# Selecting the top keys of the indexer: two of its passes over a tile moved to ScalarE, and two VectorE passes merged into one

## The chip, the cores and the metric

The kernel runs on one core of one Trainium2 chip. The metric is the device time of one execution in microseconds (us). A core has five engines that work side by side, each through its own queue in order: TensorE (PE in the rows, its weight loads PEld), VectorE (DVE), ScalarE (ACT), GpSimd (POOL) and SyncE (SP), which issues the transfers between HBM and the on-chip memory. An instruction that waits for another engine holds up everything behind it on its own queue.

## The reference

One decoder block over 1024 positions of width 1024. What matters here is the sparse branch. An indexer scores every key for every query, each query keeps its 256 best admissible keys, and attention runs over those alone:

```python
iscore = jnp.where(causal[None], iscore, -jnp.inf)
_, sel = lax.top_k(iscore, topk)          # topk = 256, ties: the lower index first
...
logits = jnp.where(valid[:, None], logits, -jnp.inf)
p = jax.nn.softmax(logits, axis=-1)
```

Beside it stand the forgetting attention ("fox", eight heads), the projections of x, two gates of 1024 columns each, an MLP of width 4096 and norms.

## The kernel before

The program is written as a list of stages, and a scheduler orders each engine's instructions by its own simulated times. What is written in one place of the program may so run among the work of another, and a change of a few instructions can reorder all that comes after it.

After the norm and the indexer's scores come 16 heads, first the eight fox heads (`n` = 0 to 7) and then the eight sparse ones. Each turn of the loop over heads holds `attention` of head n, the projection `proj_qk` (and `proj_v`) of the next head, and one or two `gate_tile` calls (table `GC`), which are pure matrix work that nothing needs soon. All matrix work goes through line L75 (`mm`); its results in the PSUM tile `g` are projections, those in `S` are attention scores, those in `pv` are probabilities times values. Transposes of probabilities go to `ptr` (L583).

The selection finds, for each query, the 256th largest score by bisection. The score is cut into a high and a low half of 16 bits each. During heads 0 to 7 `bisect_step` counts how many keys lie above a threshold, 4 bits per head; the three widest of the six key tiles are counted on ScalarE (`AF.Sign` with an accumulator, L495), the others on VectorE (L498). Query tiles 2 to 7 take part, and tile i has W = 128 (i + 1) columns, so W is 384, 512, 640, 768, 896 or 1024.

When the last bit is known, at the end of turn n = 7, `select_tile` (L521 to L535) turns each tile into a mask that holds 0 for a chosen key and 1e30 for any other. `sel[i]` holds the low halves (`L`), `isc[i]` the high ones (`hi`), `Thi`, `Tlo` the threshold, `need` the number of ties to take. `bjunk` (called `gt`) and `eqt` (`eq`) are scratch tiles of which there is one each, so the six tiles follow one another. Its passes over a tile, all on VectorE, are: L527 counts low halves above the threshold, L529 and L531 mark ties, L530 marks what is above, L532 numbers the ties in order (a running sum), L533 keeps the first `need` of them, L534 adds both marks, L535 makes the mask. L528 works on one column. The masks are first read by the sparse heads.

The scheduler interleaves these with what the fox heads want of VectorE: L563 reads attention scores out of `S` (out to `sp`, `mn`), L592 adds up a head's result from `pv` (`yt`), L585 makes the low part of transposed probabilities (`pl`), L318 and L325 read out projections (`QB`, `KA`). GpSimd meanwhile splits weights into a high and a low part (L120, L123).

Of the kernel before, what the change touches and what calls it, by code (L numbers as in the profile page):

```python
# [16 lines left out]
AF = mybir.ActivationFunctionType  # L17
ALU = mybir.AluOpType
# [14 lines left out]
BIG = 1.0e30  # L33
# [24 lines left out]
def block_kernel(ctx: ExitStack, tc: tile.TileContext, x, c, w_ada, b_ada, g_norm1, w_in, b_forget,  # L58
                 rel_bias, w_bf, w_bd, w_out, g_norm2, w_mlp1, w_mlp2, g_final, onehot, out):
    nc = tc.nc  # L60
# [49 lines left out]
    def split_w(pieces, lo_eng=None, kt=KT, dst=None):  # L110
        st = stg.tile([P, 1024], F32, name="st", tag="st")
        view = st.rearrange("p (k c) -> p k c", k=kt)
        for d0, d1, src in pieces:
            nc.sync.dma_start(view[:, :, d0:d1], src)
        return split_st(st, lo_eng, dst)
# [50 lines left out]
    isc, sel = [None, None], [None, None]  # L166
# [299 lines left out]
    cnt = pA.tile([P, NQ], F32, name="cnt")  # L466
    goal = pA.tile([P, NQ], F32, name="goal")
    nct = pA.tile([P, NQ], F32, name="nct")
# [52 lines left out]
    def select_tile(i):  # L521
        q, W = i - 2, (i + 1) * P
        hi = isc[i].bitcast(I16)[:, 1::2]
        L = sel[i].bitcast(U16)
        th, tl, nd = Thi[:, q:q + 1], Tlo[:, q:q + 1], need[:, q:q + 1]
        gt, eq = bjunk[:, :W], eqt[:, :W]
        nc.vector.tensor_scalar(gt, L, tl, None, op0=ALU.is_gt, op1=ALU.add, accum_out=cnt[:, q:q + 1])  # L527
        nc.vector.tensor_tensor(nd, nd, cnt[:, q:q + 1], op=ALU.subtract)  # L528
        nc.vector.tensor_scalar(eq, L, tl, None, op0=ALU.is_equal)  # L529
        nc.vector.scalar_tensor_tensor(gt, hi, th, gt, op0=ALU.is_gt, op1=ALU.add)  # L530
        nc.vector.scalar_tensor_tensor(eq, hi, th, eq, op0=ALU.is_equal, op1=ALU.mult)  # L531
        nc.vector.tensor_tensor_scan(out=L, data0=eq, data1=eq, initial=0.0, op0=ALU.add, op1=ALU.max)  # L532
        nc.vector.scalar_tensor_tensor(eq, L, nd, eq, op0=ALU.is_le, op1=ALU.mult)  # L533
        nc.vector.tensor_tensor(gt, gt, eq, op=ALU.add)  # L534
        nc.vector.tensor_scalar(sel[i], gt, -BIG, BIG, op0=ALU.mult, op1=ALU.add)  # L535


    def attention(kind, h, qk, V, Yd=None):
# [190 lines left out]
    for n, (kind, h) in enumerate(heads):  # L729
# [19 lines left out]
        if n == NH - 1:  # L749
            for i in range(2, NTT):  # L750
                select_tile(i)
# [23 lines left out]
    for half in range(2):  # L775
        sl = slice(half * 512, half * 512 + 512)
        for cp in range(4):
            hi, lo = split_w([(0, 256, wbv[1][:, :, cp * 256:cp * 256 + 256])], nc.gpsimd, 4)
            hv, lv = hi.rearrange("p (k c) -> p k c", k=4), lo.rearrange("p (k c) -> p k c", k=4)
            for c2 in range(2):  # L780
                ct, cs = 2 * cp + c2, slice(c2 * P, c2 * P + P)
                gt = pY.tile([P, 512], F32, name="gt2", tag="gt2", bufs=3)
# [22 lines left out]
    with ExitStack() as st4:  # L805
# [6 lines left out]
        for ch in range(2):  # L812
# [3 lines left out]
            for t in range(NTT):  # L816
                hf, tl = t // 4, slice((t % 4) * P, (t % 4) * P + P)
# [398 lines left out]
```

## Time and profile before

| | |
|---|---|
| median of 3 runs | 1632.06 us (1631.8 to 1632.16) |
| profiled execution, its own time | 1634.09 us |
| its span, first to last instruction | 1632.2 us |
| TensorE busy | 1565.2 us, 96% of the span |
| VectorE busy | 1150.7 us, 71% |
| ScalarE busy | 947.4 us, 58% |
| GpSimd busy | 747.9 us, 46% |
| mean granted clock of TensorE | 0.984 of full speed |

The profiled execution is one run more, and it is about 2 us longer than the median of the others. "Busy" of TensorE counts a matmul until its modelled end, and matmuls overlap, so it says when the engine has nothing to do and not how well it works. The selection lies at 430 to 500 us of the span.

### The profile page before, as it was taken

Reading aid. Unit: us, or ns where it says so; the run is one execution under the profiler, and the core shown is the slowest. Engines: PE = TensorE matmul, PEld = TensorE weight load, DVE = VectorE, ACT = ScalarE, POOL = GpSimd, SP = SyncE. Lnnn points to the kernel's source line nnn. Section 1 sums busy time; section 2 is a strip of 40 time slices with the busy share of each in tenths; the row PEclk is TensorE's granted clock in tenths of the full one; section 3 lists DMA queues with packets and bytes.
Section 4 is the critical chain, followed back from the end, with each engine's and each line's share of the span. In section 5 each row is a group of like instructions: output and inputs, shape, how many; then the busy total and the mean of one; then the engine's idle time right before and its main releaser. Section 6 shows DMA issues by size and latency. Waiting matters only on the chain.

```text
span 1632.2 us, 22837 instructions
## 1 busy us (share of the span) xinstructions
PE 1565.2 (96%) x7585; PEld 1300.7 (80%) x7585; DVE 1150.7 (71%) x2230; ACT 947.4 (58%) x1689; POOL 747.9 (46%) x628
## 2 busy tenths in 40 slices
PE   4989999999989999999999998999999989999998
PEld 3777788887878888888888887888888868888887
DVE  6787777878897665567767547765555475758988
ACT  4454899898747777677663136554544343533433
POOL 3432222333335565656545301886666564343730
PEclk8999999999999999999999999999999989999999
DMA  9321222132124443544878456454444579655862
GB/s 301 81 47 51 61 79 57 44 80 49 53 63 147 116 138 100 155 139 142 304 242 292 126 187 215 141 167 152 151 142 143 181 287 344 231 207 193 268 222 103
DMA packets 223870, 253.01 MB, mean 155 GB/s; under 512 B 49137, under 2 KB 136257, under 8 KB 223753
## 3 DMA queue, kind: packets, MB, share of 16 engines
q1 hardware_dynamic: 215112, 233.73, 45.5%
q10 hardware_dynamic: 8640, 17.83, 2.9%
q8 instruction: 60, 0.98, 0.3%
q14 instruction: 58, 0.47, 0.1%
HBM read 186.48 MB, written 65.03 MB: 154 GB/s over the span
## 4 chain that ended last, share of the span: by engine, by line
PE 73%; DVE 10%; ACT 9%; DMA 4%; issue 2%; SPq 1%; POOL 1%; ACTq 0%; DVEq 0%; POOLq 0%
PE g L75 31%; PE S L75 24%; PE tr L75 8%; PE pv L75 7%; ACT eqt L495 4%; PE ptr L583 2%; ACT sp L567 1%; DVE acc L252 1%; DMA wap<-in_w_ada_dram 1%; ACT sp L570 1%; ACT ph L584 1%; DVE sp L563 1%; DVE pl L585 1%; DVE isc L434 1%; DMA gt<-G_d 1%
## 5 line engine op out<-in xcount | busy, mean ns | idle before, releaser
L75 PE MATMUL g<-h_hi,whi 128*128 128x512 f32 x656 | 264.5, 403 | 8.4 <-DVE KA L325 5.4
L75 PE MATMUL g<-h_hi,wlo 128*128 128x512 f32 x656 | 262.7, 400 | 0.0
L75 PE MATMUL g<-h_lo,whi 128*128 128x512 f32 x656 | 262.5, 400 | 0.0
L1039 DVE TENSOR_TENSOR ut<-rw,ut 128x1024 fp32r<-128x1024 f32 x112 | 182.0, 1670 | 66.3 <-ACT ut L1038 66.2
L123 POOL TENSOR_TENSOR wlo<-st,whi 128x1024 fp32r<-128x1024 f32 x60 | 148.6, 2477 | 110.7 <-ACT whi L122 103.0
L1038 ACT ACTIVATE ut<-rw 128x1024 fp32r<-128x1024 f32 x112 | 112.0, 1052 | 144.7 <-PE pv L75 66.6
L1053 POOL TENSOR_TENSOR rw<-rw 128x1024 f32<-128x1024 f32 x40 | 117.6, 2943 | 125.5 <-DMA rw<-in_w_mlp_dram 114.2
L75 PEld LDWEIGHTS g<-h_hi,whi 128*128 128x128 f32 x656 | 125.2, 191 | 34.1 <-issue 5.5
L75 PEld LDWEIGHTS g<-h_hi,wlo 128*128 128x128 f32 x656 | 124.7, 190 | 24.3
L75 PEld LDWEIGHTS g<-h_lo,whi 128*128 128x128 f32 x656 | 124.9, 190 | 22.5
L75 PE MATMUL S<-ut 128*128 128x512 f32 (+1 forms) x576 | 138.4, 385 | 0.0
L75 PEld LDWEIGHTS S<-ut 128*128 128x128 f32 x576 | 106.9, 191 | 21.2 <-DVE ut L1039 0.2
L585 DVE TENSOR_TENSOR pl<-ptr,ph 128x512 fp32r<-128x512 f32 (+1 forms) x160 | 99.8, 631 | 23.6 <-ACT ph L584 21.7
L567 ACT ACTIVATE sp<-sp,mn 128x128 f32<-128x128 f32 (+7 forms) x128 | 98.5, 771 | 25.5 <-DVE mn L563 25.2
L584 ACT ACTIVATE ph<-ptr 128x512 fp32r<-128x512 f32 (+1 forms) x160 | 86.4, 550 | 42.5 <-PE ptr L583 40.5
L495 ACT ACTIVATE eqt<-sel_all,nct 128x768 bf16<-128x768 int16 (+5 forms) x99 | 102.5, 1035 | 9.9 <-DVE nct L491 8.5
L570 ACT ACTIVATE sp<-sp,mn 128x128 f32<-128x128 f32 (+7 forms) x128 | 96.9, 770 | 18.6 <-DVE mn L569 18.1
L75 PE MATMUL g<-ut 128*128 128x512 f32 (+1 forms) x384 | 94.6, 381 | 6.0 <-ACT ut L1038 4.6
L583 PE MATMUL ptr<-ident,sp 128*128 128x128 f32 x576 | 89.8, 272 | 1.6 <-DVE nct L491 1.2
L122 ACT ACTIVATE whi<-st 128x1024 fp32r<-128x1024 f32 x51 | 53.8, 1055 | 62.3 <-DMA st<-in_w_mlp_dram 18.5
L75 PE MATMUL pv<-ph,V 128*128 128x256 f32 x320 | 85.2, 285 | 3.1 <-DVE yt L592 3.1
L75 PEld LDWEIGHTS g<-ut 128*128 128x128 f32 x384 | 70.0, 191 | 20.5 <-ACT ut L1038 5.0
(436 smaller groups left out, 3922.5 us busy)
## 6 DMA issues: line engine op xcount, KB each, us to landing
rw<-in_w_mlp_dram SPq DMA_DIRECT2D x72, 512.0 KB
rw<-U_d SPq DMA_DIRECT2D x56, 512.0 KB
wap<-in_w_ada_dram SPq DMA_DIRECT2D x64, 256.0 KB
st<-in_w_mlp_dram SPq DMA_DIRECT2D x32, 512.0 KB
st<-in_w_in_dram SPq DMA_DIRECT2D x26, 512.0 KB
U_d<-cc SPq DMA_DIRECT2D x48, 256.0 KB
st<-in_w_in_dram SPq DMA_DIRECT2D x33, 256.0 KB
G_d<-t SPq DMA_DIRECT2D x32, 256.0 KB
```

Of the source, the lines that this page charges most:

```text
L75: nc.tensor.matmul(o, l, r, start=start, stop=stop)
L122: nc.scalar.activation(hi, st, AF.Copy)
L123: (lo_eng or nc.vector).tensor_tensor(lo, st, hi.bitcast(F32), op=ALU.subtract)
L495: nc.scalar.activation(eqt[:, :(i + 1) * P], sel[i].bitcast(dt), AF.Sign, bias=nct[:, q], accum_out=cnt[:, q])
L567: nc.scalar.activation(sp[:, :W], sp[:, :W], AF.Exp, bias=mn[:, len(cs) - 1:len(cs)], scale=-1.0, accum_out=mn[:, 2:3])
L570: nc.scalar.activation(sp[:, :W], sp[:, :W], AF.Copy, scale=mn[:, 3:4])
L583: nc.tensor.transpose(tr[:, n * P:(n + 1) * P], pt[s][:, kb * P:(kb + 1) * P], ident)
L584: nc.scalar.activation(ph[:, z:], tr[:, z:], AF.Copy)
L585: nc.vector.tensor_tensor(pl[:, z:], tr[:, z:], ph[:, z:].bitcast(F32), op=ALU.subtract)
L1038: nc.scalar.activation(ut[:, n], t, AF.Copy)
L1039: nc.vector.tensor_tensor(ut[:, n + 1], t, ut[:, n].bitcast(F32), op=ALU.subtract)
L1053: nc.gpsimd.tensor_tensor(o, a, b, op=op)
```

## The change

In `select_tile` the count of low halves above the threshold is made by ScalarE: `Sign` of (L - threshold - 0.5) gives -1 or +1 for each key, and its accumulated sum gives the number. For this each tile needs two more instructions of one column ahead of it (`nt` in `nct`, `nw` in `goal`) and one behind it (`nd`, which replaces L528). The mark `gt` is now -1 to +2 in place of 0 or 1, and one pass (`-eq > gt`) says which keys are left out, in place of the sum of two marks and the scaling. ScalarE multiplies this by 1e30 and writes the mask. Of passes over a tile VectorE has six after the change and eight before; ScalarE has two and had none. Nothing else is edited; the gate projections stay in the turns in which they were.

```diff
--- before.py
+++ after.py
@@ -524,15 +524,18 @@
         L = sel[i].bitcast(U16)
         th, tl, nd = Thi[:, q:q + 1], Tlo[:, q:q + 1], need[:, q:q + 1]
         gt, eq = bjunk[:, :W], eqt[:, :W]
-        nc.vector.tensor_scalar(gt, L, tl, None, op0=ALU.is_gt, op1=ALU.add, accum_out=cnt[:, q:q + 1])
-        nc.vector.tensor_tensor(nd, nd, cnt[:, q:q + 1], op=ALU.subtract)
+        nt, nw = nct[:, q:q + 1], goal[:, q:q + 1]
+        nc.vector.tensor_scalar(nt, tl, -1.0, -0.5, op0=ALU.mult, op1=ALU.add)
+        nc.vector.tensor_scalar(nw, nd, float(W // 2), None, op0=ALU.subtract)
+        nc.scalar.activation(gt, L, AF.Sign, bias=nt, accum_out=cnt[:, q:q + 1])
         nc.vector.tensor_scalar(eq, L, tl, None, op0=ALU.is_equal)
-        nc.vector.scalar_tensor_tensor(gt, hi, th, gt, op0=ALU.is_gt, op1=ALU.add)
         nc.vector.scalar_tensor_tensor(eq, hi, th, eq, op0=ALU.is_equal, op1=ALU.mult)
         nc.vector.tensor_tensor_scan(out=L, data0=eq, data1=eq, initial=0.0, op0=ALU.add, op1=ALU.max)
+        nc.vector.scalar_tensor_tensor(nd, cnt[:, q:q + 1], -0.5, nw, op0=ALU.mult, op1=ALU.add)
+        nc.vector.scalar_tensor_tensor(gt, hi, th, gt, op0=ALU.is_gt, op1=ALU.add)
         nc.vector.scalar_tensor_tensor(eq, L, nd, eq, op0=ALU.is_le, op1=ALU.mult)
-        nc.vector.tensor_tensor(gt, gt, eq, op=ALU.add)
-        nc.vector.tensor_scalar(sel[i], gt, -BIG, BIG, op0=ALU.mult, op1=ALU.add)
+        nc.vector.scalar_tensor_tensor(gt, eq, -1.0, gt, op0=ALU.mult, op1=ALU.is_gt)
+        nc.scalar.activation(sel[i], gt, AF.Copy, scale=BIG)
 
 
     def attention(kind, h, qk, V, Yd=None):
```

From L527 on the line numbers shift: L563 is L566 after the change, L585 is L588, L592 is L595, L583 is L586, L584 is L587, L567 is L570, L570 is L573, L591 is L594. L318, L325, L313 and L320 keep theirs. Inside the new `select_tile` L530 is the Sign pass on ScalarE, L531 to L533 and L535 to L537 are VectorE's six passes, L528, L529 and L534 the narrow instructions, L538 the Copy on ScalarE.

All five queues hold the same order as before up to the end of the bisection and again, but for single rows, from the last part of the sparse branch on (some 4350 of TensorE's 7535 rows in, at about 880 us of the span before). Between the two the scheduler has reordered them, mostly by a few rows; no other instruction is added or lost. Three places follow.

The first is VectorE's queue in the tile of 896 columns. It begins with the read-out of the last attention scores of this fox head and ends with the projection read-out `KA`. Before:

```order
L563 ISA sp,mn<-S,cmask,mn 128x512
L563 ISA mn 128x1
L535 TENSOR_SCALAR sel_all<-bjunk 128x768
L529 TENSOR_SCALAR eqt<-sel_all,Tlo 128x896
L318 SCALAR_TENSOR_TENSOR QB<-g,QA 64x512
L527 TENSOR_SCALAR bjunk,cnt<-sel_all,Tlo 128x896
L531 SCALAR_TENSOR_TENSOR eqt<-isc,Thi,eqt 128x896
L569 RECIPROCAL mn<-mn 128x1
L528 TENSOR_TENSOR need<-need,cnt 128x1
L592 TENSOR_TENSOR yt<-pv,yt 64x256
L530 SCALAR_TENSOR_TENSOR bjunk<-isc,Thi,bjunk 128x896
L325 TENSOR_TENSOR KA<-g,KA 64x512
```

After:

```order
L566 ISA sp,mn<-S,cmask,mn 128x512
L566 ISA mn 128x1
L532 SCALAR_TENSOR_TENSOR eqt<-isc,Thi,eqt 128x896
L318 SCALAR_TENSOR_TENSOR QB<-g,QA 64x512
L533 SCALAR_TENSOR_TENSOR sel_all<-eqt 128x896
L534 SCALAR_TENSOR_TENSOR need<-cnt,goal 128x1
L535 SCALAR_TENSOR_TENSOR bjunk<-isc,Thi,bjunk 128x896
L572 RECIPROCAL mn<-mn 128x1
L536 SCALAR_TENSOR_TENSOR eqt<-sel_all,need,eqt 128x896
L595 TENSOR_TENSOR yt<-pv,yt 64x256
L588 TENSOR_TENSOR pl<-ptr,ph 128x512 x2
L325 TENSOR_TENSOR KA<-g,KA 64x512
```

Both pieces hold the second mark of ties (L531, now L532) and the first half of `QB`. Ahead of `yt` stood the mask of tile 768, the first mark, the count and the narrow instruction of this tile; now the running sum, the mark of what is above and the choice of ties stand there, and two `pl` are between `yt` and `KA`.

The second is TensorE's queue at the matmuls that wait for this `yt` (first `pv`) and this `KA` (first `g` behind it). Before:

```order
L75 MATMUL g<-h_lo,whi 128x512
L75 MATMUL g<-h_hi,wlo 128x512
L75 MATMUL pv<-ph,V 128x256
L75 MATMUL g<-h_hi,whi 128x512
L75 MATMUL g<-h_lo,whi 128x512
```

After:

```order
L75 MATMUL g<-h_hi,wlo 128x512
L75 MATMUL pv<-ph,V 128x256
L75 MATMUL pv<-pl,V 128x256
L75 MATMUL pv<-ph,V 128x256
L75 MATMUL pv<-pl,V 128x256
L75 MATMUL pv<-ph,V 128x256
L586 MATMUL ptr<-ident,sp 128x128 x3
L75 MATMUL pv<-pl,V 128x256
L75 MATMUL pv<-ph,V 128x256
L75 MATMUL pv<-pl,V 128x256
L586 MATMUL ptr<-ident,sp 128x128 x4
L75 MATMUL g<-h_hi,whi 128x512
```

One matmul of `pv` stood between the projections; now eight and seven transposes stand there, of which all but that one came later before. The nine projections that stood between the last attention scores (`S`, 384 columns) and this `pv` are ahead of those scores now, but for one.

The third is ScalarE's queue over the same stretch. Before:

```order
L570 ACTIVATE sp<-sp,mn 128x768
L593 ACTIVATE yh<-yt 64x256
L567 ACTIVATE sp,mn<-sp,mn 128x896
L313 ACTIVATE QA<-g 64x512
L570 ACTIVATE sp<-sp,mn 128x896
L567 ACTIVATE sp,mn<-sp,mn 128x1024
L591 ACTIVATE yt<-pv 64x256
L320 ACTIVATE KA<-g 64x512
```

After:

```order
L570 ACTIVATE sp,mn<-sp,mn 128x896
L538 ACTIVATE sel_all<-bjunk 128x768
L313 ACTIVATE QA<-g 64x512
L573 ACTIVATE sp<-sp,mn 128x896
L530 ACTIVATE bjunk,cnt<-sel_all,nct 128x896
L570 ACTIVATE sp,mn<-sp,mn 128x1024
L594 ACTIVATE yt<-pv 64x256
L587 ACTIVATE ph<-ptr 128x512 x2
L320 ACTIVATE KA<-g 64x512
```

The Copy of tile 768 and the Sign of tile 896 now stand among the attention work; the instructions around them keep their order.

## Rows read from the trace of the kernel before

**Rows 1.** Busy time by stretch: PE, PEld, DVE, ACT, POOL, granted clock, DMA share, GB/s.

```profile
430.00:476.00 46.00, 39.19 (x201) 32.01 (x199) 45.67 (x98) 23.86 (x48) 17.26 (x19) 1.00 0.17 44
476.00:480.00 4.00, 4.00 (x11) 3.19 (x12) 4.00 (x4) 0.00 (x0) 3.86 (x3) 0.59 0.07 16
...
600.00:700.00 100.00, 97.70 (x530) 83.89 (x529) 53.68 (x146) 66.26 (x132) 60.45 (x66) 0.98 0.46 135
780.00:960.00 180.00, 178.90 (x873) 147.95 (x872) 112.90 (x215) 81.99 (x136) 75.25 (x52) 1.00 0.70 232
```

**Rows 2.** Timeline of TensorE, matmuls that it had to wait for; in brackets the idle time.

```profile
446.32 0.47 PE L75 MATMUL g<-h_hi,whi 128*128 128x512 f32 x1 [1.52 <-DVE KA L325]
...
457.79 0.44 PE L75 MATMUL S<-KA,QA 128*128 128x384 f32 x1 [0.89 <-DVE mn L563]
...
469.94 0.44 PE L75 MATMUL S<-KA,QA 128*128 128x384 f32 x1 [1.48 <-DVE mn L563]
...
474.21 0.36 PE L75 MATMUL pv<-ph,V 128*128 128x256 f32 x1 [1.57 <-DVE yt L592]
...
475.90 0.50 PE L75 MATMUL g<-h_hi,whi 128*128 128x512 f32 x1 [1.34 <-DVE KA L325]
```

**Rows 3.** Chain that ended last, pieces in order of time: start, us, what.

```profile
475.90 6.69 PE g L75 x21
...
484.18 4.13 PE g L75 x18
...
795.37 0.96 PE pv L75 x8
796.33 0.77 PE ptr L583 x7
```

**Rows 4.** Source lines of select_tile; ns minimum, median and maximum of the six tiles.

```profile
L527 DVE TENSOR_SCALAR_CACHE_REDUCE bjunk<-sel_all,Tlo x6: 596/933/1274, 430.8 to 485.5; 128x384 bf16<-128x384 uint16 x1, 128x512 bf16<-128x512 uint16 x1, 128x640 bf16<-128x640 uint16 x1, 128x768 bf16<-128x768 uint16 x1
...
L528 DVE TENSOR_TENSOR need<-need,cnt x6: 139/149/1759, 432.2 to 489.0; 128x1 f32<-128x1 f32 x6
...
L530 DVE SCALAR_TENSOR_TENSOR bjunk<-isc,Thi,bjunk x6: 608/942/1279, 432.2 to 489.1; 128x384 bf16<-128x384 int16 x1, 128x512 bf16<-128x512 int16 x1, 128x640 bf16<-128x640 int16 x1, 128x768 bf16<-128x768 int16 x1
...
L534 DVE TENSOR_TENSOR bjunk<-bjunk,eqt x6: 353/550/993, 438.3 to 494.8; 128x384 bf16<-128x384 bf16 x1, 128x512 bf16<-128x512 bf16 x1, 128x640 bf16<-128x640 bf16 x1, 128x768 bf16<-128x768 bf16 x1
...
L535 DVE TENSOR_SCALAR sel_all<-bjunk x6: 239/325/3186, 439.1 to 496.3; 128x384 bf16<-128x384 bf16 x1, 128x512 bf16<-128x512 bf16 x1, 128x640 bf16<-128x640 bf16 x1, 128x768 bf16<-128x768 bf16 x1
```

**Rows 5.** Timeline of VectorE, 457 to 477 us: what TensorE waits for.

```profile
457.26 0.47 DVE L563 CUSTOM_DVE_ANT_0 sp<-S,cmask,mn 128x256 f32<-128x256 f32 x1
...
469.15 0.72 DVE L563 CUSTOM_DVE_ANT_0 sp<-S,cmask,mn 128x512 f32<-128x512 f32 x1
...
473.65 0.41 DVE L592 TENSOR_TENSOR yt<-pv,yt 64x256 f32<-64x256 f32 x1
...
475.15 0.69 DVE L325 TENSOR_TENSOR KA<-g,KA 64x512 fp32r<-64x512 f32 x1
...
476.49 2.08 DVE L532 TENSOR_TENSOR_SCAN sel_all<-eqt 128x896 uint16<-128x896 bf16 x1
```

**Rows 6.** Timelines of GpSimd and then VectorE, long instructions that lie side by side.

```profile
440.49 2.73 POOL L123 TENSOR_TENSOR wlo<-st,whi 128x1024 fp32r<-128x1024 f32 x1
...
454.25 2.40 POOL L123 TENSOR_TENSOR wlo<-st,whi 128x1024 fp32r<-128x1024 f32 x1
...
476.78 3.97 POOL L123 TENSOR_TENSOR wlo<-st,whi 128x1024 fp32r<-128x1024 f32 x1
...
441.47 1.76 DVE L528 TENSOR_TENSOR need<-need,cnt 128x1 f32<-128x1 f32 x1
...
454.76 2.57 DVE L533 SCALAR_TENSOR_TENSOR eqt<-sel_all,need,eqt 128x640 bf16<-128x640 uint16 x1
```

**Rows 7.** Group of ScalarE, 400 to 430 us: Sign passes; busy us, mean ns | idle.

```profile
L495 ACT ACTIVATE eqt<-sel_all,nct 128x768 bf16<-128x768 uint16 (+2 forms) x12 | 12.4, 1035 | 0.0
```

**Rows 8.** Waits of TensorE, 640 to 720 us: total, times, longest.

```profile
PE g L75 <- DVE t L668: 2.3, 1, 2.3
```

## Prediction

> **What bounds the kernel now.** The view of busy time by stretch comes first [rows 1]. At 430 to 476 us, where the selection runs among the last fox head, VectorE is busy 45.67 of 46 us and TensorE only 39.19, while ScalarE has 23.86 and so 22 us to spare. From 476 us on TensorE is busy all the time until past 600 us, and loses 2.3 us of the next hundred and 1.1 us of 780 to 960. So VectorE bounds 46 us and TensorE what follows; what VectorE gives back later than 476 us is hidden under TensorE.
>
> What TensorE loses there is told by the five matmuls that waited [rows 2]: 1.52 us for `KA`, 0.89 and 1.48 us for a read-out of scores, 1.57 us for `yt`, 1.34 us for `KA`: 6.8 us, all for VectorE. The chain shows what comes on top: 21 projections from 475.90 took 6.69 us where 18 took 4.13 us a little later [rows 3], 0.229 each, so 21 of them would be 4.8 us. The 1.9 us too much is the clock, granted at 0.59 of full speed at 476 to 480 us [rows 1], which is between the two levels of 1.2 and 2.4 GHz, after TensorE had been idle for half of the time since 468. The prize is thus 6.8 + 1.9 = 8.7 us at most in this stretch.
>
> The timeline shows one thing more about VectorE [rows 6]. Two of its instructions took far longer than they do alone: L528, one column, 1.76 us beside a median of 0.149 [rows 4], and L533 at 640 columns 2.57 us, where the like pass L530 takes 608 to 1279 ns for 384 to 1024 columns, so about 0.88. Each lies beside a weight split on GpSimd (L123 at 440.49 and 454.25 us) and ends within 0.7 us of its end. These waits took 1.6 and 1.7 us.
>
> **What VectorE saves.** Six counts go (L527, median 933 ns), but six merged passes come that are of L530's kind (942 ns): nothing either way. What is saved are L534 and L535 [rows 4]. Their medians are 0.55 and 0.325 us, and as an instruction starts some 0.07 us before the one ahead of it ends, six of each occupy the queue for 6 x (0.875 - 0.14) = 4.4 us. Twelve narrow instructions are added (18 for 6). L528 shows 0.149 us each; overlapped it is 0.08, so they cost 0.9 to 1.8 us. I take 0.9, since they follow one another without a wait. VectorE is relieved of 3.5 us in all, much less than the words "two passes moved" suggest, and more than half of that lies in the tiles of 896 and 1024 columns, which end after the last wait of TensorE.
>
> **What ScalarE takes on.** A Sign pass over 768 to 1024 columns took 1.035 us [rows 7]; over these six widths it is about 0.9, and a Copy I set at the same, so 11 us, which 22 us of idle time cover. No row shows a Copy from and to 16 bits; between nothing for what is covered, and half a microsecond for each tile where VectorE has to wait for ScalarE (below), I take the wait at one tile only. The rule of the Trainium skill's page "ScalarE: Activation LUTs", section Rules for kernel authors, speaks against this move: simple arithmetic belongs on VectorE, which is up to about three times as fast in bf16. The rows agree on the ratio (L535 0.325 us, Sign 1.035 us); by the rule alone the change would cost some 9 us of engine time net, by the idle time of ScalarE nothing.
>
> **What the path gets of it.** I follow VectorE's queue to the last two matmuls that waited, since what counts is when `yt` and `KA` come.
> - To the read-out at 457.26 us [rows 5]: the first tile now has the added narrow instructions of all tiles in front and loses 0.4 us, the second gains 0.45, the third has gained its count, 0.8. The read-out comes 0.85 us earlier, if both waits beside GpSimd come back at the same price. Bounds: 4.2 us earlier if neither comes back, 0.5 us later if both last the whole of a split (2.73 and 2.40 us).
> - From there to `yt`, 16.39 us before. What goes by rows 4, interpolated by width and less the overlap: L534 and L535 of 640 and of 768 columns, the counts of 768 and 896, L528 twice; 4.1 us with the 0.99 us that one L534 took. What comes: the merged passes of 640 and 768, the running sum of 896 (2.08 us, 2.0 less overlap) [rows 5], its mark and its choice of ties, which used to stand behind `yt`: 0.8 + 0.94 + 2.0 + 2 x 1.07 = 5.9. So 1.75 us longer. The running sum also overwrites what the Sign pass reads, and Copy of 768, `QA`, a softmax scaling and Sign of 896 are in ScalarE's queue ahead of it: about 3.5 us against 3.0 us of VectorE's own work, so 0.45 us of waiting (0 to 1). Together 2.2 us.
> - `KA` then waits behind two `pl` more. TensorE fills that time with eight matmuls of `pv` and seven transposes which it used to do later, 0.96 + 0.77 = 1.7 us [rows 3], to be taken off.
>
> The sum at the gate where TensorE runs free again: -0.85 + 2.2 - 1.7 = -0.35 us. The waits for scores and for the first `KA` should nearly go, and come back as one long wait of about 6 us for `yt`. The clock then falls as before, so its 1.9 us I leave (0 to 3.8). VectorE ends its selection 3 us or more earlier than at 499.5, and nobody waits for that. For the reordered stretch up to 880 us I take no change: TensorE idles little there, so there is less to win (2.3 us with what the clock lost) [rows 8] than to lose.
>
> The profiled execution took 1634.09 us, 2.03 more than the median; 1634.09 - 0.35 = 1633.74, against the median 1631.7.
>
> **The rivals.**
> *The locks miss.* The two waits beside GpSimd do not recur, because the order around them is new. That takes 3.3 us more off the path: 1628.4; if the clock also stays up, 1626.5. For it: L123 starts when its own inputs are there, and VectorE's work beside it is reordered. Against it: nearly all passes that are left read two tiles, like L533, and the count that went is not among those that the rows show held up.
>
> *A lock before `yt`.* GpSimd's next split (3.97 us from 476.78) [rows 6] now finds `yt` and `KA` still waiting behind the running sum and two passes, where before both were done. If it comes in ahead of them, they wait 2.4 to 4.0 us more: 1634.1 to 1635.7, say 1635.2. It decides from 3.6 us on. Against it: the split follows `KA` through GpSimd's own copy of it, so it is itself late when `KA` is. The Trainium skill's page "SBUF — State Buffer", section Who interferes with whom, has this as a rule: a VectorE instruction with two inputs in SBUF and a GpSimd instruction that reads SBUF shut each other out for a whole instruction, while the accumulating form does not take part. By that rule the change removes the one pass that can't be held up, and the time tends to this rival; rows 6 agree on the price, 1.6 and 1.7 us.
>
> *A new wait in the reordered stretch.* At 600 to 700 us TensorE waited once 2.3 us for a gate tile that came late from HBM (L668) [rows 8] and the clock was 0.98 over 100 us, 2 us more [rows 1]. One more such wait among heads 8 to 15 or at the start of the sparse branch's output projection costs 4.3 us: 1636.0. It decides alone from 3.6 us. For it: 450 us of queues are reordered, SP's among them. Against it: most rows move by a few places.
>
> **How the numbers follow.** 0.2% is 3.3 us, about what a measurement of this kernel can tell from no change. I give my forecast 0.5, the missed locks 0.2, the lock before `yt` 0.14, the new wait 0.16. Faster by over 0.2% (below 1628.8): the missed locks, nearly all; 0.2. Slower (above 1635.3): the new wait, half of the lock, and some of the forecast's own spread; 0.29. Within: 0.51. The range goes from the missed locks with part of the clock, 1627, to the new wait and a little, 1637.5; my forecast's own range, by the bounds on ScalarE's wait and the locks, is 1629.5 to 1634.
>
> **What would show it right or wrong.** VectorE's time in the six passes and the narrow instructions is 3 to 4 us less than the old nine lines took without their waits. Busy time of TensorE at 430 to 480 us stays near 43 us of 50, with one gap of 5 to 7 us before a `pv`, released by `yt` (L595), and granted clock well below full speed behind it. VectorE waits for ScalarE (L530) under 1 us in all but one tile. If the gap is gone or under 3 us, and the waits before it too, the path got the relief and I am wrong; if TensorE waits over 2 us anywhere at 500 to 900 us where it did not, the order is what decides.

## The result, and the profile of the changed kernel

The changed kernel takes 1643.04 us (median of five, 1639.46 to 1644.2) beside 1632.16 for the kernel before: a ratio of 1.0061, 95% interval 1.0047 to 1.0076, so 10 to 11 us slower. The prediction was 1631.7 us, with a range of 1627 to 1637.5. It was wrong.

The profiled execution took 1644.2 us. Its span is 1642.2 us, 10.0 us longer than that of the kernel before, and 1.8 us of this were there before the selection began (the end of the bisection, L518, moved from 430.04 to 431.81 us). Where the rest went is seen when losses are counted along the matmuls. The traces of the two programs hold the same 7585 rows of TensorE, so each can be given a price: the median time from its start to the next start, for its tile names and its width, in the trace of before. What a row takes above that is loss, whether TensorE waited or its clock was low. Summed over the same amounts of work, which in the trace of before end at 431, 511, 765 and 919 us:

| us lost by TensorE | to 431 | 431 to 511 (selection) | 511 to 765 | 765 to 919 | rest |
|---|---|---|---|---|---|
| before | 41.3 | 9.9 | 4.3 | 3.8 | 19.0 |
| changed | 43.3 | 13.1 | 0.1 | 13.9 | 18.1 |

So the selection itself lost 3.2 us more, the one wait at 687 us [rows 8] is gone and gave 4.2 us back, and the last heads lost 10.1 us more. The last two numbers lie where no pass of the selection runs. The view of busy time by stretch shows the same, to be held against [rows 1]; its columns are those named there:

```profile
430.00:454.00 24.00, 24.00 (x127) 20.28 (x126) 21.27 (x54) 15.89 (x37) 9.44 (x14) 1.00 0.11 28
454.00:458.00 4.00, 1.35 (x7) 0.79 (x5) 4.00 (x3) 0.00 (x0) 2.41 (x1) 0.96 0.74 180
458.00:466.00 8.00, 7.73 (x26) 6.66 (x27) 8.00 (x18) 5.09 (x10) 0.00 (x0) 0.59 0.20 60
474.00:478.00 4.00, 1.49 (x7) 0.96 (x6) 4.00 (x5) 3.71 (x8) 2.67 (x3) 1.00 0.00 0
478.00:486.00 8.00, 6.21 (x24) 5.50 (x25) 7.84 (x15) 5.23 (x11) 4.80 (x4) 0.57 0.08 17
600.00:700.00 100.00, 100.00 (x550) 86.20 (x549) 58.09 (x154) 68.09 (x140) 66.01 (x70) 1.00 0.48 137
768.00:880.00 112.00, 104.58 (x546) 87.39 (x545) 71.17 (x156) 65.61 (x121) 60.02 (x54) 0.97 0.74 242
```

Up to 454 us TensorE now has no gap: the wait for the first `KA` is gone, as was forecast. Then it has two long ones, 454 to 458 and 474 to 482 us, in place of five short ones, and behind each the granted clock is near 0.6 over 8 us, where before it fell once, over 4 us. The next row shows that 600 to 700 us run without a loss at full clock (0.98 before). The last row holds the loss: 104.58 us busy of 112, at a clock of 0.97. The timeline of TensorE has the waits, the answer to [rows 2]:

```profile
458.27 0.58 PE L75 MATMUL S<-KA,QA 128*128 128x256 f32 x1 [2.92 <-DVE mn L566]
...
479.79 0.55 PE L75 MATMUL pv<-ph,V 128*128 128x256 f32 x1 [4.30 <-DVE yt L595]
...
780.10 0.72 PE L75 MATMUL g<-isc,whi 128*128 128x512 f32 x2 [1.05 <-DVE t L671]
...
786.76 0.50 PE L75 MATMUL g<-h_hi,whi 128*128 128x512 f32 x1 [2.02 <-DVE t L671]
...
808.05 0.73 PE L75 MATMUL g<-isc,whi 128*128 128x512 f32 x2 [0.96 <-DVE t L671]
...
875.40 1.22 PE L75 MATMUL S<-Yd,whi 128*128 128x512 f32 x2 [2.83 <-DVE gt L792]
```

The timelines of GpSimd and of VectorE show what made the first two, beside [rows 5, 6]:

```profile
444.05 2.40 POOL L123 TENSOR_TENSOR wlo<-st,whi 128x1024 fp32r<-128x1024 f32 x1
...
452.32 1.04 POOL L120 CAST whi<-st 128x1024 fp32r<-128x1024 f32 x1 [5.87 <-PE g L75]
...
453.61 2.79 POOL L123 TENSOR_TENSOR wlo<-st,whi 128x1024 fp32r<-128x1024 f32 x1
...
474.98 1.83 POOL L120 CAST whi<-st 128x1024 fp32r<-128x1024 f32 x1 [1.14 <-PE g L75]
...
479.86 2.36 POOL L123 TENSOR_TENSOR wlo<-st,whi 128x1024 fp32r<-128x1024 f32 x1
...
444.77 2.75 DVE L533 TENSOR_TENSOR_SCAN sel_all<-eqt 128x512 uint16<-128x512 bf16 x1 [0.76 <-ACT bjunk L530]
...
452.39 0.98 DVE L534 SCALAR_TENSOR_TENSOR need<-cnt,goal 128x1 f32<-128x1 f32 x1
...
454.09 3.66 DVE L533 TENSOR_TENSOR_SCAN sel_all<-eqt 128x640 uint16<-128x640 bf16 x1
...
460.01 0.47 DVE L566 CUSTOM_DVE_ANT_0 sp<-S,cmask,mn 128x256 f32<-128x256 f32 x1
...
475.90 0.93 DVE L534 SCALAR_TENSOR_TENSOR need<-cnt,goal 128x1 f32<-128x1 f32 x1
...
479.23 0.41 DVE L595 TENSOR_TENSOR yt<-pv,yt 64x256 f32<-64x256 f32 x1
```

The running sums of 512 and 640 columns (L533) took 2.75 and 3.66 us. Before, with no split beside them, they took 1.30 and 1.48. They end 1.07 and 1.35 us behind the end of a split that began ahead of them (446.45 and 456.40 us), which is about the time that they take alone: they waited for the whole split. Two instructions on one column (L534) ended in the same way with a cast on GpSimd. Such a wait of one engine until the other's instruction ends is called a lock here. So the locks came back at 1.45, 2.18, 0.84 and 0.8 us, where 1.6 and 1.7 had been. What that adds up to is seen in the groups of VectorE, 429 to 506 us (busy us, mean ns | idle and what ended it):

```profile
L533 DVE TENSOR_TENSOR_SCAN sel_all<-eqt 128x384 uint16<-128x384 bf16 (+5 forms) x6 | 13.4, 2236 | 1.0 <-ACT bjunk L530 1.0
...
L537 DVE SCALAR_TENSOR_TENSOR bjunk<-eqt,bjunk 128x384 bf16<-128x384 bf16 (+5 forms) x6 | 5.3, 878 | 0.0
...
L534 DVE SCALAR_TENSOR_TENSOR need<-cnt,goal 128x1 f32<-128x1 f32 x6 | 2.5, 411 | 0.0
```

The six running sums took 13.4 us, and VectorE stood idle 1.0 us ahead of them for ScalarE's Sign pass; in e4 below, where two of them met no split, they took 10.4. The merged pass cost what L530 does, as priced (0.88 us).

### The profile page after: what moved, and what is told of

Read it like the earlier page. It is cut to its first block, busy times and chain, and to the rows that moved or that the text cites. A ratio compares the mean times of both kernels' runs of the same rounds, so it can differ in the third digit from the quotient of the medians.

```text
span 1642.2 us, 22849 instructions
## 1 busy us (share of the span) xinstructions
PE 1570.9 (96%) x7585; PEld 1306.3 (80%) x7585; DVE 1139.5 (69%) x2224; ACT 956.0 (58%) x1707; POOL 741.2 (45%) x628
## 4 chain that ended last, share of the span: by engine, by line
PE 74%; DVE 10%; ACT 10%; DMA 3%; issue 2%; SPq 1%; POOL 1%; ACTq 0%; DVEq 0%; POOLq 0%
PE g L75 31%; PE S L75 24%; PE tr L75 8%; PE pv L75 7%; ACT eqt L495 4%; PE ptr L586 2%; DVE acc L252 1%; ACT sp L570 1%; ACT sp L573 1%; ACT ph L587 1%; DVE bjunk L498 1%; DVE sp L566 1%; DVE pl L588 1%; DVE isc L434 1%; DVE cand L516 1%
## 5 line engine op out<-in xcount | busy, mean ns | idle before, releaser
L123 POOL TENSOR_TENSOR wlo<-st,whi 128x1024 fp32r<-128x1024 f32 x60 | 145.9, 2432 | 136.5 <-ACT whi L122 124.2
L1056 POOL TENSOR_TENSOR rw<-rw 128x1024 f32<-128x1024 f32 x40 | 113.8, 2849 | 127.9 <-DMA rw<-in_w_mlp_dram 117.1
L570 ACT ACTIVATE sp<-sp,mn 128x128 f32<-128x128 f32 (+7 forms) x128 | 98.5, 770 | 34.1 <-DVE mn L566 34.0
L588 DVE TENSOR_TENSOR pl<-ptr,ph 128x512 fp32r<-128x512 f32 (+1 forms) x160 | 99.6, 631 | 24.2 <-ACT ph L587 23.0
L587 ACT ACTIVATE ph<-ptr 128x512 fp32r<-128x512 f32 (+1 forms) x160 | 86.1, 550 | 38.7 <-PE ptr L586 33.7
L573 ACT ACTIVATE sp<-sp,mn 128x128 f32<-128x128 f32 (+7 forms) x128 | 96.9, 770 | 15.5 <-DVE mn L572 15.2
L586 PE MATMUL ptr<-ident,sp 128*128 128x128 f32 x576 | 90.4, 275 | 1.5 <-DVE nct L491 1.2
L75 PE MATMUL pv<-pl,V 128*128 128x256 f32 x320 | 84.4, 290 | 3.0 <-DVE pl L588 1.8
```

The costliest lines, as they stand in the source:

```text
L75: nc.tensor.matmul(o, l, r, start=start, stop=stop)
L123: (lo_eng or nc.vector).tensor_tensor(lo, st, hi.bitcast(F32), op=ALU.subtract)
L570: nc.scalar.activation(sp[:, :W], sp[:, :W], AF.Exp, bias=mn[:, len(cs) - 1:len(cs)], scale=-1.0, accum_out=mn[:, 2:3])
L573: nc.scalar.activation(sp[:, :W], sp[:, :W], AF.Copy, scale=mn[:, 3:4])
L586: nc.tensor.transpose(tr[:, n * P:(n + 1) * P], pt[s][:, kb * P:(kb + 1) * P], ident)
L587: nc.scalar.activation(ph[:, z:], tr[:, z:], AF.Copy)
```

## The experiments

Two theories were on the table. **A, the order:** most of the loss belongs to the order in which the scheduler put the instructions that the change doesn't touch, and the selection's own share to what its passes stand ahead of, and to locks. **B, the work:** ScalarE's two passes and passes that can be locked out are dear wherever they stand.

To part them, orders had to be held fast. The scheduler takes edges that ask only for order of issue. A kernel that chains every instruction of a queue to the next by such edges runs in that order, and the selection's instructions are either chained too or left for the scheduler to place:

```diff
+ORDER = (
...
+def pin(tc, nc):
...
+        for k in seq[p + 1:p + 1 + n]:
+            i = ins[new[k]]
+            if prev is not None:
+                tc.add_manual_dep(i, prev.name, info, reason="order")
+            prev = i
...
         block_kernel(tc, *args)
+        pin(tc, nc)
```

In the traces of e4, e5, e6, e11 and e12, which keep the changed kernel's order, TensorE's queue holds the changed kernel's rows one for one, and in e1 it holds those of the kernel before. Each group of runs was timed beside the kernel before, whose medians were 1633.26 us (e1 to e4), 1633.34 (e5 to e8), 1632.75 (e9 and e10) and 1633.71 (e11 and e12); ratios are to these. The losses of all runs, counted as above:

| us lost by TensorE | to 431 | 431 to 511 | 511 to 765 | 765 to 919 | rest |
|---|---|---|---|---|---|
| e1 new passes, old order | 41.8 | 11.4 | 3.9 | 5.3 | 18.8 |
| e2 old passes, new order | 41.1 | 13.8 | 0.1 | 13.2 | 19.2 |
| e3 old passes, narrow added | 43.0 | 9.1 | 0.7 | 10.4 | 20.1 |
| e4 changed, splits as zeros | 40.0 | 7.7 | 0.1 | 13.9 | 19.9 |
| e5 changed, more buffers | 41.7 | 13.3 | 0.1 | 11.9 | 19.2 |
| e6 changed, splits in parts | 41.2 | 10.9 | 0.1 | 13.4 | 18.7 |
| e7 new passes, urgent first | 39.8 | 6.9 | 2.0 | 3.7 | 17.8 |
| e8 e7 with e5 and e6 | 41.2 | 4.9 | 1.3 | 4.2 | 18.0 |
| e9 as e8, old passes | 42.3 | 8.6 | 1.6 | 3.8 | 19.1 |
| e10 e8 again | 40.9 | 4.9 | 1.9 | 4.6 | 18.8 |
| e11 changed, loads early | 42.6 | 13.2 | 0.1 | 11.1 | 19.3 |
| e12 changed, e5, e6 and e11 | 43.4 | 10.8 | 0.1 | 11.0 | 18.4 |

The first column is work that no kernel changes, and it moves by up to 3.6 us from one execution to another. That is why the medians, not one execution, carry the verdicts, and why the table is read column by column. The profiled executions of the changed kernel, e1, e3 and e10 are the slowest of their runs, that of e12 is 3.2 us above its median, and that of e7 is its fastest. The column of 765 to 919 us is steadier: it holds 3.7 to 5.3 us in the six rows with the order of before (the kernel before, e1 and e7 to e10), and 13.2 to 13.9 in those with the new order and no repair there (the changed kernel, e2, e4 and e6).

### Order against work: e1 and e2

`select_tile` of one kernel, the order of the other. The edit is `pin` with the other kernel's ORDER.

> The changed select_tile, with every other instruction of all five queues held in the order that it has in the kernel before; only the selection's own instructions are placed freely among them. In the two profiled executions the changed kernel loses 10 us: about 1.7 us were lost before the selection begins, about 3 us more in 430 to 490 us (a wait of 2.92 us for a read-out, one of 4.30 us for yt, and the granted clock at 0.50 to 0.69 twice in place of once), and about 6 us more in 480 to 880 us (six waits of 0.4 to 2.8 us for transfers, against one of 2.3 us and three short ones). Theory A, the order: the 6 us belong to the new order of the queues behind the selection, so they go: 1634 us, 1632 to 1636. Theory B, the work: two passes on ScalarE and the passes that VectorE can be locked out of are dear in any order: 1639 us or more.

> The other half: select_tile of the kernel before, with every other instruction in the order of the changed kernel. Theory A: the waits for transfers at 770 to 880 us are there as in the changed kernel, and the selection costs about what it cost before: 1638 us, 1636 to 1642. Theory B: the order costs nothing by itself: 1632 to 1634 us.

Measured: e1 1633.88 us, ratio 1.0004 (0.9994 to 1.0014). e2 1643.23 us, ratio 1.0067 (1.0054 to 1.0081). The old passes in the new order are as slow as the changed kernel, and the new passes in the old order as fast as the kernel before. Theory B falls as the cause of the 10 us. e2 came out above the 1636 to 1642 us of Theory A, which had let the selection cost what it cost before. The timeline of TensorE in e2, where not one pass of the selection is new:

```profile
455.98 0.63 PE L583 MATMUL ptr<-ident,sp 128*128 128x128 f32 x4 [4.25 <-DVE V L344]
...
479.63 0.55 PE L75 MATMUL pv<-ph,V 128*128 128x256 f32 x1 [4.59 <-DVE yt L592]
...
785.46 0.50 PE L75 MATMUL g<-h_hi,whi 128*128 128x512 f32 x1 [1.63 <-DVE t L668]
...
874.08 1.22 PE L75 MATMUL S<-Yd,whi 128*128 128x512 f32 x2 [2.81 <-DVE gt L789]
```

These are the changed kernel's waits, at the same places, but for the first, which is for `V` in place of the read-out. Even the selection's own loss (13.8 us) comes with the new order. The expectation counted six waits for transfers in the last heads of the changed kernel; there are five waits, the four of its timeline above and one of 0.37 us at 828 us, which is for ScalarE.

### A new order by a trifle: e3

```diff
         gt, eq = bjunk[:, :W], eqt[:, :W]
+        nt, nw = nct[:, q:q + 1], goal[:, q:q + 1]
+        nc.vector.tensor_scalar(nt, tl, -1.0, -0.5, op0=ALU.mult, op1=ALU.add)
+        nc.vector.tensor_scalar(nw, nd, float(W // 2), None, op0=ALU.subtract)
         nc.vector.tensor_scalar(gt, L, tl, None, op0=ALU.is_gt, op1=ALU.add, accum_out=cnt[:, q:q + 1])
```

> The kernel before with nothing of the change but its twelve narrow instructions ahead of the passes, whose results nobody reads; VectorE gets 0.9 us more to do and no pass moves. The scheduler reorders about as many rows behind the selection as the change does (1762 of TensorE's, against 1869). Theory A, a new order is a draw that no pass decides: the time may lie anywhere from 1627 to 1645 us, and whatever it loses or wins lies in waits for transfers at 600 to 900 us. Theory B: 1632 to 1633.5 us.

Measured: 1635.07 us, ratio 1.0015 (1.0005 to 1.0025). The median alone leaves it open: 2 us is little more than the 0.9 us of work. The table shows more: 3.6 us were won at 511 to 765 us and 6.6 us lost at 765 to 919, by twelve instructions of one column at 430 us. That the time came out near that of before is the luck of this order.

### The locks: e4 and e6

Both keep every queue of the changed kernel in its order. e4 writes zeros in the three splits, so that the low parts of three weights are missing from the result. e6 splits in four parts and leaves nothing out.

```diff
+        if no_lo[0]:
+            nc.gpsimd.memset(lo.bitcast(F32), 0.0)
+        else:
+            (lo_eng or nc.vector).tensor_tensor(lo, st, hi.bitcast(F32), op=ALU.subtract)
```

```diff
+        w = 1024 // parts[0]
+        for c in range(parts[0]):
+            cs = slice(c * w, c * w + w)
+            (lo_eng or nc.vector).tensor_tensor(lo[:, cs], st[:, cs], hi[:, cs].bitcast(F32), op=ALU.subtract)
```

> The changed kernel with every queue in its own order, but the three weight splits of GpSimd that lie in the selection (the low parts of the projections of head 8 and of one gate tile) write zeros in place of the difference, so that GpSimd reads no SBUF there; the low parts of these three weights are left out of the result. In the changed kernel the running sums of 512 and 640 columns took 2.75 and 3.66 us beside such splits, 1.45 and 2.2 us more than the 1.30 and 1.48 us that they take alone. Theory A (locks are most of what the stretch lost): the wait of 2.92 us for the read-out goes to under 1 us, and with it the low clock behind it: 3 to 5 us faster than the changed kernel, 1638 to 1640. Rival: the splits only lie beside the running sums, which are late for ScalarE's Sign pass: within 1 us of the changed kernel, 1642 to 1644.

> The changed kernel in its own order, with the three weight splits of GpSimd that lie in the selection done in four instructions of 256 columns each, nothing left out. If VectorE and GpSimd keep each other out for one instruction at a time, the running sums should wait for about 0.6 us in place of up to 2.2: the wait for the read-out at 458 us shrinks as in the run with zeros, and the time falls by 3 to 5 us, to 1638 to 1640. Rival: if GpSimd holds on as long as its next part is ready, nothing is won: 1642 to 1644.

Measured: e4 1637.17 us, ratio 1.0022 (1.0009 to 1.0036), 5.9 us faster than the changed kernel by the medians and 6.4 by the ratios, and more than was expected of it. e6 1639.57 us, ratio 1.0041 (1.0027 to 1.0054), 3.5 us faster by the medians and 3.3 by the ratios. The running sums of 512 and 640 columns fell to 1.23 and 1.48 us in e4 and to 1.78 and 2.03 in e6. The timelines of VectorE, GpSimd and TensorE in e6:

```profile
451.95 2.03 DVE L539 TENSOR_TENSOR_SCAN sel_all<-eqt 128x640 uint16<-128x640 bf16 x1
...
451.47 4.42 POOL L127 TENSOR_TENSOR wlo<-st,whi 128x256 fp32r<-128x256 f32 x4
...
476.19 0.55 PE L75 MATMUL pv<-ph,V 128*128 128x256 f32 x1 [6.67 <-DVE yt L601]
```

Here four parts took 4.42 us where a split takes 2.4: the two engines took turns, and the running sum lost half a microsecond, about a part, in place of two. In both runs the wait for the read-out shrank (to nothing, and to 1.29 us); the one for `yt` stayed, at 5.69 and 6.67 us. That one is mostly the queue, as forecast: of locks ahead of `yt` e4 shows only 1.0 us (the running sum of 896 columns took 2.74 us in place of 2.02, and L539, the choice of ties, 1.42 in place of 1.14).

### What stands ahead of what: e7 to e10

e7 has the new passes in the old order, as e1, but the placing of the passes isn't left to the scheduler's times: some stand behind rows that TensorE waits for. e8 adds the parts of e6 and the buffers of e5 (below). e9 is e8 with the eight old passes. e10 is e8 once more, on the chip of e9.

```diff
             for i in range(2, NTT):
                 select_tile(i)
+            for t, which, k in LATE:
+                BEHIND.extend((names[11 * t + w], k) for w in which)
...
+    for name, k in BEHIND:
+        tc.add_manual_dep(ins[name], new[k], info, reason="order")
```

> The changed select_tile with every other instruction in the order of the kernel before, as in the first run, but with the selection's passes held behind what TensorE waits for: the running sum of 512 columns behind KA, the choice of ties of 640 behind the read-out of scores, the last two passes of 768 behind the last read-out, all of 896 behind yt and the first half of KA, all of 1024 behind its second half. The first run still lost about 7.2 us of TensorE's time there (1.92, 0.49, 1.23 and 3.57 us and low clock). If VectorE's order decides: 1628 to 1631 us, clear of the kernel before. If the selection's length decides, the masks only come later and head 8 waits for them: 1633 to 1636.

> The last kernel with the splits in four parts and the gate tiles in the two scratch tiles as well. If each of the three is worth what its theory says, they add: the one wait of 2.3 us at 687 us and its low clock may go too; 1622 to 1628 us. If two of them take from the same wait: 1628 to 1631.

> The eight VectorE passes of the kernel before, nothing on ScalarE, in the order of the kernel before, with the three edits of the last kernel: passes held behind what TensorE waits for, splits in four parts, gate tiles in the scratch tiles. It differs from the last kernel only by the change itself. If VectorE's relief of some 3.5 us reaches TensorE once the order is right, this is 2 to 4 us slower than the last kernel: 1628 to 1630 against 1625.5. If order and locks are all that counts, the two are within 1 us of each other.

> The kernel with the six passes and all three edits once more, on the same chip as its counterpart with eight passes: 1624 to 1627 us, 0.4 to 0.6% faster than the kernel before.

Measured: e7 1630.37 us, ratio 0.9982 (0.9969 to 0.9994); e8 1625.54, ratio 0.9952 (0.9935 to 0.9969); e9 1630.28, ratio 0.9985 (0.9974 to 0.9996); e10 1624.71, ratio 0.9945 (0.9931 to 0.9958). e8 beats both kernels, by 7.8 and 17.5 us of the medians. What is left of waits in it, in the timeline of TensorE, and the clock of the stretch:

```profile
458.92 0.33 PE L592 MATMUL ptr<-ident,sp 128*128 128x128 f32 x1 [0.91 <-ACT sp L579]
...
470.15 0.38 PE L75 MATMUL pv<-ph,V 128*128 128x256 f32 x1 [0.50 <-ACT ph L593]
...
479.28 0.47 PE L75 MATMUL g<-h_hi,whi 128*128 128x512 f32 x1 [1.43 <-DVE KA L331]
```

```profile
460.00:480.00 20.00, 18.07 (x93) 14.73 (x92) 19.84 (x34) 14.37 (x26) 8.88 (x9) 1.00 0.15 39
480.00:500.00 20.00, 20.00 (x109) 17.10 (x108) 17.14 (x36) 13.32 (x29) 9.86 (x13) 1.00 0.54 151
```

No gap is longer than 1.43 us, and the clock stays at full speed. Held against e9, which has but the old passes, the change is worth 5.6 us (1630.28 to 1624.71), where 2 to 4 were expected: this is the relief that the prediction couldn't find at TensorE. In e9 VectorE reaches this `KA` 4 us later than in e8 (1.1 of them lost before the selection), and the granted clock of 480 to 500 us is 0.91:

```profile
483.51 0.47 PE L75 MATMUL g<-h_hi,whi 128*128 128x512 f32 x1 [3.93 <-DVE KA L331]
```

### The last heads: e5, e11 and e12

Why are transfers late at 770 to 880 us? The queue of SyncE in the changed kernel (start us, time on the queue, what it issues):

```profile
771.18 0.38 SPq L114 DMA_DIRECT2D st<-in_w_branch_fox_dram  x1
771.65 0.46 SPq L672 DMA_DIRECT2D M_d<-t  x1
...
776.27 0.33 SPq L667 DMA_DIRECT2D t<-G_d  x1
...
780.07 0.33 SPq L672 DMA_DIRECT2D M_d<-t  x1
...
782.15 0.32 SPq L667 DMA_DIRECT2D t<-G_d  x1
...
866.82 0.22 SPq L646 DMA_DIRECT2D R_d<-arow  x1
...
869.18 1.29 SPq L787 DMA_DIRECT2D gt<-G_d  x3
```

and in the kernel before:

```profile
771.51 0.33 SPq L669 DMA_DIRECT2D M_d<-t  x1
772.11 0.38 SPq L114 DMA_DIRECT2D st<-in_w_branch_fox_dram  x1
773.66 0.91 SPq L664 DMA_DIRECT2D t<-G_d  x2
...
857.24 0.23 SPq L643 DMA_DIRECT2D R_d<-arow  x1
...
857.85 1.52 SPq L784 DMA_DIRECT2D gt<-G_d  x3
```

A gate is loaded (L667, L664 before) when an earlier one has been stored (L672) and its buffer is free. Here the store at 771.65 took 4.56 us to land, and the next load was issued right then. The store was late itself, by one row of the new order: the load of a weight (L114, `st`) now stands ahead of it and waited 3.0 us for a split on GpSimd (L123), while the result to be stored was ready at 769.69 us (L671); before, the store stood ahead of that load. No run moves this row alone. The last three gates (`gt`, at 869.18 and 857.85) stand behind the rows of `arow` (`R_d`). In the new order they are issued 11 us later, while TensorE is only 6 us late there by the count along its matmuls. e5 gives the first kind two more buffers, e11 issues the second kind ahead of the first `R_d<-arow` (three places moved in ORDER) into three more, and e12 does both and the parts of e6, all in the changed kernel's order otherwise.

```diff
-            g = pQ.tile([P, 512], F32, name="t512", tag="t512", bufs=3)
+            if c2 == 0:
+                g = (bjunk, eqt)[n % 2].bitcast(F32)
+            else:
+                g = pQ.tile([P, 512], F32, name="t512", tag="t512", bufs=3)
...
-                gt = pY.tile([P, 512], F32, name="gt2", tag="gt2", bufs=3)
+                gt = pY.tile([P, 512], F32, name="gt2", tag="gt2", bufs=6)
```

> The changed kernel in its own order, but every second gate tile of branch_fox (t) lies in one of the two scratch tiles of the selection, which are free by then, in place of the three t512 buffers that it shares with the other gates and the projections. In the changed kernel the loads t<-G_d at 776 and 782 us start right when an earlier store M_d<-t has landed (771.65 + 4.56 and 780.07 + 2.06 us), and TensorE waits 1.05, 2.02 and 0.96 us for the results made of them, with low clock and the queue behind. Theory A (the waits are for a free buffer): these waits go, 3 to 5 us faster than the changed kernel, 1638 to 1640. Rival (the loads are late by their place in SP's queue, or by the traffic of the DMA engines): within 1 us, 1642 to 1644.

> The changed kernel in its own order but for three rows of SP's queue: the loads gt<-G_d of 869.18 us stand ahead of the first store R_d<-arow (861.35 us), into three buffers more (six of gt2 in place of three), so that they neither wait behind the two arow rows nor for the passes that free the old buffers. In the changed kernel the last of the three landed at 874.57 us, TensorE waited 2.83 us for what is made of them and then ran at a granted clock of 0.59 for some 6 us. Theory A (TensorE has too little work left behind the last sparse head to cover these loads): wait and low clock go, 4 to 5.5 us faster than the changed kernel: 1637.5 to 1639. Rival: the loads of mf or the read-out take over as the last to come: under 2 us.

> The changed kernel in its own order with all three repairs of single waits: splits in four parts, gate tiles in the two scratch tiles, the three loads early. Alone the first gave 3.5 us, the second 1.4, the third should give 4 to 5.5. If they add: 1633 to 1635, the time of the kernel before, with the order that cost 10 us left as it is. If something in the order itself is left that no single wait shows: 1636 or more.

Measured: e5 1641.65 us, ratio 1.0048 (1.003 to 1.0067), 1.4 us faster than the changed kernel by the medians and 2.1 by the ratios, where 3 to 5 were expected. Two of its three waits for `t` shrank (1.05 us to nothing, 2.02 to 0.67), the third stayed (1.00). e11 1641.44 us, ratio 1.0043 (1.0027 to 1.0058), 1.6 us by the medians and 2.9 by the ratios, where 4 to 5.5 were expected. e12 1636.28 us, ratio 1.0014 (1.0002 to 1.0027), 6.8 us by the medians and 7.7 by the ratios. The three gave 6.5 and 8.3 alone, so they add within the noise, and e12 misses its 1633 to 1635 us mainly because e11 gave so little. e11 shows what happened, in the timelines of TensorE, VectorE, GpSimd and SyncE:

```profile
882.90 0.72 PE L75 MATMUL S<-Yd,whi 128*128 128x512 f32 x2 [1.54 <-DVE gt L794]
...
873.28 5.22 DVE L795 TENSOR_TENSOR gt<-gt,mf 128x512 f32<-128x512 f32 x2
...
872.74 2.42 POOL L729 TENSOR_TENSOR wol<-st,woh 128x1024 fp32r<-128x1024 f32 x1 [0.60 <-ACT woh L728]
875.11 2.84 POOL L123 TENSOR_TENSOR wlo<-st,whi 128x1024 fp32r<-128x1024 f32 x1
...
878.53 0.32 SPq L790 DMA_DIRECT2D mf<-M_d  x1
878.90 1.37 SPq L789 DMA_DIRECT2D gt<-G_d  x3
```

The wait of 2.83 us at 875 us is gone, and the next one comes 7 us later, for the next three gates. In between, two passes of VectorE (L795) took 5.22 us, where they take 1.28 in the changed kernel (L793 at 878.29 us): moved forward, they lie beside two splits on GpSimd. The load of `mf` is issued as the second of them ends (878.51 us), and the next gates stand right behind it on the queue, only 1.5 us earlier than in the changed kernel (880.40 us). So here mending one wait moved it to the next, by way of a lock; what this lock costs, no run isolates. In the table, 765 to 919 us lose 13.9 us in the changed kernel, 11.9 with e5, 11.1 with e11 and 11.0 with both; these are single executions, and since the medians add, it isn't shown that the two repairs take from the same loss. What is left, 11 us where the old order loses about 4, no repair explains. A reading that is argued and not shown is that the new order has TensorE spend its other work too early, so that too little is left to cover the chain of transfers behind the last sparse heads. Which rows of the order make up the whole loss stays open; no run puts one queue alone back into the old order.

## Why the prediction was wrong, step by step

**"For the reordered stretch up to 880 us I take no change": this step failed,** by 5.9 us (4.2 won at 687 us, 10.1 lost at 765 to 919). The argument was that TensorE idles little there, so there is less to win than to lose, and the step then took nothing for the loss. The rival of a new wait had the right place and kind, a gate tile late from HBM with low clock behind, but one wait of 4.3 us and a chance of 0.16. Five waits came, four of them for gate tiles; they sum to 7.2 us, where three before summed to 1.1, and behind the last the granted clock was 0.63 (875 to 883 us). e2 and e3 show that such a loss needs no change in the selection's passes at all.

**The clock ("as before, its 1.9 us I leave, 0 to 3.8") failed next.** TensorE's waits in the selection come to 2.92 + 4.30 = 7.2 us, beside 6.8 before, close to the one long wait that was forecast. But they came as two long gaps, each with a low clock behind it: (1 - 0.59) x 7.73 = 3.2 and (1 - 0.57) x 6.21 = 2.7 us by the rows above, where the kernel before lost (1 - 0.59) x 4.00 = 1.6. That is 4.3 us more of clock, more than the 3.2 us by which the selection's loss grew; what the count holds beside waits and clock went from 1.5 us to nothing.

**The head start at the read-out (-0.85 us) came out at +1.0** (460.01 less 1.77 less 457.26). That is beyond its bound of 0.5 us later. The price of the locks was wrong: the running sums met both splits almost from their start and lost 1.45 and 2.18 us, and L534 lost 0.84 to a cast, 4.5 us in all where 3.3 were taken. And the wait for ScalarE's Sign pass, set at 0.45 us ahead of `yt`, was 0.76 us in the tile of 512, ahead of the read-out, and 0.26 in that of 896.

**From the read-out to `yt`: +2.2 us forecast, +2.8 measured** (19.22 beside 16.39 us), right in kind: the running sum and two passes of 896 columns stand there. That it came so near in size is partly luck, since 1.1 us of it are L534 and L536 beside casts (0.93 and 1.42 us, alone 0.15 and 1.14), which the forecast did not have. **The matmuls moved forward** filled as forecast: no wait for `KA` is left, and the one for `yt` was 4.30 us where some 6 were expected. The lock before `yt` didn't come; the split began at 479.86 us, just behind it.

**What VectorE saves** was taken somewhat too small: 3.5 us forecast, 5.3 measured in e9 and e10, where the lines of `select_tile` sum to 47.1 and 41.8 us. Both sums hold locks; with the shortest time that each instruction shows in any run they are 40.8 and 36.3, so 4.5 us. ScalarE's part was right (11 us, measured 11.1). The rule of the page "ScalarE: Activation LUTs" of the Trainium skill, section Rules for kernel authors, would have left the multiplication on VectorE, and the count too if Sign, which it doesn't name, is read into it; e9 and e10 differ by 5.6 us the other way, since VectorE is the full engine here.

**The rival of missed locks** is what e4 ran: with the locks on the splits gone the time was 1637 and not 1628 us; 5.9 of these 9 us are the order's, lost in the last heads less what was won at 687 us.

## What to carry to other kernels

Where a scheduler orders queues by its own times, the first cost of an edit is a new order of everything behind it. Judge the edit and the order apart: hold the old order fast and put the new code into it, and the other way about. A loss in a stretch that the edit doesn't touch, as here after 765 us, is the sign. And relief on a full engine is worth what stands first in its queue: the same six passes ran at 1.0004 of the kernel before where the scheduler put them (e1), and at 0.9982 behind the rows that TensorE waits for (e7).

## What the runs showed of the hardware

Running sums on VectorE wait for a whole split on GpSimd (3.66 and 2.75 us, and 1.48 and 1.23 in e4, where GpSimd writes zeros and reads nothing there), and for about a part of it when it comes in four (2.03 and 1.78). The section Who interferes with whom of the Trainium skill's page "SBUF — State Buffer" says that one of the two engines takes a shared pair of ports for a whole instruction and the other blocks; these runs agree.

In these rows nearly the same idle time cost more clock when it came in fewer pieces: five waits of 0.89 to 1.57 us cost 1.6 us of clock before, two of 2.92 and 4.30 us cost 5.9 us after; in e8, with waits of 0.50 to 1.43 us, the granted clock stayed at 1.00, the level of 2.4 GHz.
